# Zero-padded operands for two small matmuls, and weight rings of 3 and 5 buffers in place of 4 and 4

## Chip, core and metric

The kernel runs on one core of a Trainium2 chip. A core has five engines with a queue each: TensorE (PE, with PEld for its weight loads), VectorE (DVE), ScalarE (ACT), GpSimd (POOL) and SyncE (SP), which here only issues DMAs. The metric is the device time of one launch, the median of several runs.

## What is computed

One inference step of a two-layer decoder of width 2048, for 256 prompt tokens and 8 sequences of 8 new tokens ("sample"), 320 tokens in all, in float32. Layer 0 is gated linear attention with 4 heads, layer 1 is spatial gating; a squared-ReLU MLP of width 8192 and a LayerNorm follow each. What the change touches is, in the reference:

```python
# gated linear attention; per head a key width of 256 and a value width of 512
s_new = exp(b_last)[..., None] * s + einsum('bhsk,bhkv->bhkv', k_to_end, v)   # per sequence
# spatial gating over chunks of 128 positions, 8 groups of features
w_causal = where(causal, w_spatial, 0.0)
mixed = einsum('gts,bnsgd->bntgd', w_causal, v_chunks) + b_spatial
out = (u * mixed) @ w_out
```

## The kernel before

Activations lie feature-major: 16 tiles of 128 features, with the 320 tokens on the free axis. Every large product is made of three matmuls (`mm3`, L139 to L141), since each operand is split into an exact high part and a low part: low weights by high activations, high by low, high by high.

Weights come in **units** of 4 feature tiles by 256 columns (512 KB). There are 736 of them; each feeds 24 matmuls of 320 columns. `unit` issues the load on SP into `raw` (3 buffers), lets ACT write the high part `wh` (L128) and DVE the low part `wl` (L129):

```python
raw = wraw.tile([P, UK, UN], F32, tag="raw", ...)
hi = ring.pool.tile([P, UK, UN], F32R, tag="h" + ring.tag, ...)
lo = ring.pool.tile([P, UK, UN], F32R, tag="l" + ring.tag, ...)
...
nc.sync.dma_start(raw[:, ks, :], src[:, ks, :])                                  # L127
nc.scalar.copy(hi[:, ks, :], raw[:, ks, :])                                      # L128
nc.vector.tensor_sub(lo[:, ks, :], raw[:, ks, :], hi[:, ks, :].bitcast(F32))     # L129
```

`hi` and `lo` come from a **ring**, a pool whose buffers are used in turn: a unit can be cast when TensorE has done its last matmul on the unit that had the buffer. While the heads are at work there is one ring (pool `wa`, 4 buffers). When they are done (`second_half`), their tiles are given back, and a second ring (pool `wb`, 4 buffers) takes turns with the first for the rest of the program.

`group` makes two or four feature tiles of a product over all 16 feature tiles of the input, in PSUM banks called `mm`. **Side work** is handed out in steps between its units. For a head (`Head`) the order is: keys and queries together (8 units), values (8), the gate r (8). Beside r's units, and beside the next head's keys and queries, runs the attention itself, in four other PSUM banks called `gl`: `prompt_scores` (L461, L467), `prompt_o` (L482, L483), `prompt_state` (L498) and, for each of 8 sequences and 2 key tiles, `sample_step`: split a state tile into `sth` and `stl` (L537 on ACT, L538 on DVE), multiply the queries `qm` by both (L540, 128 rows by 512 columns), and work out what the state gains (L543) for DVE to add (L545). For L543 a sequence's keys are 32 rows of the tile `kts` (8 tokens by four parts) and its values the same 32 rows of `vts`, so the matmul contracts 32 rows:

```python
nc.tensor.matmul(pu[:], hd.kts[32 * i : 32 * (i + 1), g, kt * P : (kt + 1) * P],
                 hd.vts[32 * i : 32 * (i + 1), g, :], start=True, stop=True)     # L543
```

`kts` is written once for each key tile, by DVE (L382), from the transposed keys in a `gl` bank; ACT copies the prompt's part of that bank to `ktp` (L381). `qd`, `kte`, `kip`, `kis` (L359 to L386) are the decayed queries and keys that DVE makes out of the `mm` banks when keys and queries are there; they need the gates' exponents (`gate_logits`, `gate_sums`, `gate_decays`), a chain over TensorE, ACT and DVE that the first head has to wait for.

In layer 1, `mix` takes one of 16 feature tiles of v at a time: it transposes the two prompt blocks (L874) and the 64 sample tokens (L875), ACT copies them to `vt` (L878) and `vs` (L879), and TensorE multiplies them by the spatial weights `wsT` (L882, twice, float32) and by `wss` (L883), which holds the sample's 64 by 64 block-diagonal weights. Float32 matmuls are two matmuls each in the profile.

At the start POOL clears the tiles `scp`, `scs`, `scst` and `qm` (L230 to L237), and makes the identity and the causal masks (L210 to L222), which DVE turns into `mask_p` (L215) and `mask_s` (L227). x comes in pairs of feature tiles and is split as the weights are (`xh` L200, `xl` L201).

The order of the instructions on each engine is set by a scheduler that works on a model of the engines: it can put a unit's matmuls ahead of another's and moves side work between them. Waits between engines follow from the tiles.

Of the kernel before, what the change touches and what calls it, by code (L numbers as in the profile page):

```python
# [8 lines left out]
F32 = mybir.dt.float32  # L9
# [6 lines left out]
P = 128  # L16
D = 2048
KT = D // P          # feature tiles of a model-width activation
TP = 256             # prompt tokens
DB, DS = 8, 8        # sample batch and new tokens  # L20
T = TP + DB * DS     # tokens side by side on the free axis
TW = T + 2           # with two columns for the gain and the offset of a norm
H = 4
DK, DV = 256, 512
CH = 64              # GLA chunk
# [5 lines left out]
UK = 4               # k tiles in a weight unit  # L31
UN = 256             # columns in a weight unit
NU = KT // UK

# columns of the per-feature vectors
# [6 lines left out]
class Ring:  # L42
    """Where the split weight units of a GEMM live."""
# [5 lines left out]
class Side:  # L49
    """Work beside a GEMM, handed out in steps over the weight units still to come."""  # L50
# [16 lines left out]
def step_kernel(ctx: ExitStack, tc: tile.TileContext, A):  # L67
# [7 lines left out]
    # ------------------------------------------------------------ pools  # L75
# [3 lines left out]
    wa = ctx.enter_context(tc.tile_pool(name="wa", bufs=4))  # L79
# [9 lines left out]

    def mmtile(n=T):  # L90
        """Of the banks for products; two more of them once the heads are done."""
        if mx is not None:
            banks[0] = (banks[0] + 1) % 6
        return (mx if banks[0] > 3 else mm).tile([P, n], F32, tag="mm", name=nm("mm"), padded_shape=[P, 512])
# [4 lines left out]
    # ------------------------------------------------------------ constants  # L99
# [16 lines left out]
    # ------------------------------------------------------------ weights  # L116
    def unit(w, row0, q, col0, ring):
        """UK k tiles of UN columns, as exact high and low parts."""
# [5 lines left out]
        step = 2 if units[0] <= 2 else UK  # the first ones in parts, for an early start  # L124
# [18 lines left out]
    def group(w, row0, cols, rh, rl, evict, side=None, width=T, before=None):  # L143
        """Two feature tiles of w[row0:row0+D].T @ x for each of cols, k tiles outermost in units."""
# [15 lines left out]
    def rsqrt(out, src, scale, eps, eps_t, pool):  # L160
        """1 / sqrt(scale * src + eps): the table's value and a Newton step."""
# [10 lines left out]
    # ------------------------------------------------------------ layer 0: GLA  # L172
# [3 lines left out]
    def bigtile(tag, dt, name):  # L176
        """A model-wide activation in one of four buffers; b1 comes with the later pool."""
        return (lp if tag == "b1" else big).tile([P, KT, TW], dt, tag=tag, name=nm(name))

# [11 lines left out]
    # x, by k tiles, and its parts  # L191
    xT = A["xT"].rearrange("(k p) t -> p k t", p=P)
    def load_x(q):
        """x for quarter q of the features."""
# [12 lines left out]
    # causal masks: prompt [s of a 128-block, (t | t of the second block)]; sample [(i, part, s), (i', t)]  # L207
# [20 lines left out]
    # where the masked scores and the sample's queries go; what they leave is zero  # L228
# [5 lines left out]
    nc.gpsimd.memset(scst[:].bitcast(F32), 0.0)  # L234
    QW = P + DS
    qm = gp.tile([P, 2, DB * QW], F32R, tag="qm", name="qm")
    nc.gpsimd.memset(qm[:].bitcast(F32), 0.0)  # L237
    # per head: [1, d1, d1 d2 | 1, d2] for the queries, [d1 d2 d3, d2 d3, d3, 1] for the keys
# [8 lines left out]
    def load_gates():  # L247
        """The gate's weights; the second ones by 32 rows: high parts (twice), low parts."""
# [7 lines left out]
    def low_gate():  # L256
        """rows 0-15 x @ w_hi, rows 16-31 x @ w_lo, [hi | lo] side by side in the stationary operand; three times"""
# [22 lines left out]
    def bc4(ap):  # L280
        """[P, 64] sample columns -> [P, 8, 4, 8], the same for each part."""
        return ap.rearrange("p (b o t) -> p b o t", b=DB, o=1)
# [4 lines left out]
    class Head:  # L287
        """The gates of a head, its k, q and v, and what GLA reads of them."""
# [5 lines left out]
        def tiles(hd):  # L294
# [6 lines left out]
            hd.kts = gp.tile([P, 2, DK], F32R, tag="kts", name=nm("kts"))  # L301
# [3 lines left out]
        def gate_logits(hd):  # L305
            """exp(-|z|) and min(z, 0) of the logits z; a step for each table of ScalarE."""
# [12 lines left out]
        def gate_sums(hd):  # L319
            """log_sigmoid(z) = min(z, 0) - ln(1 + exp(-|z|)), summed along the chunks."""  # L320
# [35 lines left out]
        def ev_k(hd, kt, ps):  # L356
# [25 lines left out]
            nc.vector.tensor_copy(hd.kts[:, :, cs], pt[:, TP:].rearrange("p (b f) -> p b f", f=P))  # L382
# [31 lines left out]
        def project_kq(hd, side, before=None):  # L414
            """k and q together, as all four tiles of the other heads' work beside it are there."""
# [25 lines left out]
        def weigh(hd):  # L441
            """o * g * silu(r)"""
# [5 lines left out]
        def finish(hd):  # L448
            """... over the root of the mean square"""
# [4 lines left out]
        def prompt_scores(hd):  # L454
            """Scores of all chunk pairs at once, [s, t] for each block of 128 keys."""
# [64 lines left out]
        def sample_first(hd):  # L520
            """rows: 64 of the queries' high parts, 64 of the low ones"""
# [7 lines left out]
        def sample_step(hd, b, kt):  # L529
            """What state tile (b, kt) adds to o, and its update."""  # L530
# [8 lines left out]
            for part in (stl, sth):  # L539
# [3 lines left out]
            nc.tensor.matmul(pu[:], hd.kts[32 * i : 32 * (i + 1), g, kt * P : (kt + 1) * P],  # L543
                             hd.vts[32 * i : 32 * (i + 1), g, :], start=True, stop=True)
# [25 lines left out]
        def steps(hd):  # L570
            """GLA, by steps: the prompt at once, the sample's sequences one by one."""
# [22 lines left out]
    # ------------------------------------------------------------ the rest: residual stream z  # L594
# [7 lines left out]
    def second_half():  # L602
        """The heads are done: their tiles make room for the residual stream."""
# [10 lines left out]
        wb = ctx.enter_context(tc.tile_pool(name="wb", bufs=4))  # L614
# [408 lines left out]
```

## Time and profile before

| | before |
|---|---|
| time, median of 3 runs (lowest, highest) | 2784.06 us (2784.03, 2784.24) |
| span of the profiled execution | 2783.4 us |
| time around that span, against the median | 0.7 us |
| TensorE busy | 2763.0 us |
| DVE, ACT busy | 1543.0, 1179.7 us |
| mean granted TensorE clock | 0.999 |
| HBM read, written | 409.60, 22.02 MB |

In rows of groups, "128\*128" behind a matmul's tiles are its rows and columns of weights, "xN" the count, then the busy time and the mean length in ns, then the idle time of the engine ahead of them. In rows in order of time, the first number is the start from the span's begin and the second the length, both in us; a bracket tells of idle time ahead and what ended it. In rows of waits: who, for whom, us in total, times, longest.

The heads take the stretch from about 40 to 480 us, layer 0's products and MLP follow, `mix` runs between 1626 and 1705 us, and the rest is layer 1's products and MLP.

### The profile page before, as it was taken

The numbers are of one execution on the slowest core, as the hardware profiler recorded it, in microseconds if no ns is written. First come the engines' busy times: TensorE is split into PE (matmuls) and PEld (weight loads), VectorE is DVE, ScalarE is ACT, GpSimd is POOL, SyncE is SP. The second block draws the span as 40 slices with busy tenths as digits, with TensorE's granted clock in tenths as the row PEclk, the third lists the DMA queues.
The fourth block names the chain that finished last, engine by engine and source line by source line (L and its number), as shares of the span: only waits on it lengthen the run. The fifth ranks groups of instructions, "written<-read, shape, count | busy, mean of one in ns | idle before, by whom it ended". The sixth has DMA issues, their size and how long they took to land.

```text
span 2783.4 us, 44616 instructions
## 1 busy us (share of the span) xinstructions
PE 2763.0 (99%) x18493; PEld 2714.9 (98%) x18493; DVE 1543.0 (55%) x2276; ACT 1179.7 (42%) x1698; POOL 52.6 (2%) x83
## 2 busy tenths in 40 slices
PE   8999999999999999999999999999999999999998
PEld 8898998999999999999999999999999999999998
DVE  6566566886444444444468764587444444444446
ACT  5545454555334324323435553455324323423433
POOL 1000000000000000000000000000000000000001
PEclk9999999999999999999999999999999999999999
DMA  6556565654444445444445444445444444444442
GB/s 221 167 190 227 152 212 190 208 156 152 148 149 152 147 149 151 147 149 151 148 137 175 149 136 126 148 144 152 150 147 151 150 147 151 150 146 151 150 147 75
DMA packets 126396, 434.52 MB, mean 156 GB/s; under 512 B 13681, under 2 KB 17905, under 8 KB 126193
## 3 DMA queue, kind: packets, MB, share of 16 engines
q1 hardware_dynamic: 118800, 407.29, 47.3%
q0 software_dynamic: 6512, 23.20, 2.4%
q8 instruction: 144, 2.36, 0.3%
q10 hardware_dynamic: 880, 1.18, 0.1%
q14 instruction: 60, 0.48, 0.1%
HBM read 409.60 MB, written 22.02 MB: 155 GB/s over the span
## 4 chain that ended last, share of the span: by engine, by line
PE 98%; DVE 0%; ACT 0%; DMA 0%; issue 0%; SPq 0%; ACTq 0%; DVEq 0%
PE mm L139 31%; PE mm L141 31%; PE mm L140 31%; PE gl L540 1%; PE gl L543 1%; PE gl L498 1%; DMA xr<-xT 0%; PE gl L882 0%; PE gl L482 0%; PE gl L883 0%; ACT z L956 0%; DMA raw<-gla_w_in 0%; PE gl L874 0%; PE gl L483 0%; PE gl L409 0%
## 5 line engine op out<-in xcount | busy, mean ns | idle before, releaser
L129 DVE TENSOR_TENSOR wl<-raw,wh 128x1024 fp32r<-128x1024 f32 (+1 forms) x738 | 900.5, 1221 | 991.5 <-ACT wh L128 988.9
L128 ACT CAST wh<-raw 128x1024 fp32r<-128x1024 f32 (+1 forms) x738 | 771.4, 1046 | 1258.3 <-PE mm L141 1140.6
L141 PE MATMUL mm<-yh,wh 128*128 128x320 f32 x2368 | 734.0, 310 | 0.0
L140 PE MATMUL mm<-yl,wh 128*128 128x320 f32 x2368 | 732.4, 310 | 0.0
L139 PE MATMUL mm<-yh,wl 128*128 128x320 f32 x2368 | 727.8, 310 | 0.0
L141 PE MATMUL mm<-hh,wh 128*128 128x320 f32 x2048 | 635.3, 310 | 0.0
L139 PE MATMUL mm<-hh,wl 128*128 128x320 f32 x2048 | 634.4, 310 | 0.0
L140 PE MATMUL mm<-hl,wh 128*128 128x320 f32 x2048 | 633.6, 309 | 0.0
L140 PEld LDWEIGHTS mm<-yl,wh 128*128 128x128 f32 x2368 | 447.0, 189 | 0.2
L141 PEld LDWEIGHTS mm<-yh,wh 128*128 128x128 f32 x2368 | 446.1, 188 | 0.1
L139 PEld LDWEIGHTS mm<-yh,wl 128*128 128x128 f32 x2368 | 444.5, 188 | 0.0
L140 PEld LDWEIGHTS mm<-hl,wh 128*128 128x128 f32 x2048 | 386.7, 189 | 0.0
L141 PEld LDWEIGHTS mm<-hh,wh 128*128 128x128 f32 x2048 | 385.8, 188 | 0.0
L139 PEld LDWEIGHTS mm<-hh,wl 128*128 128x128 f32 x2048 | 385.8, 188 | 0.0
L139 PE MATMUL mm<-xh,wl 128*128 128x320 f32 x768 | 246.4, 321 | 9.7 <-ACT xh L200 5.8
L140 PE MATMUL mm<-xl,wh 128*128 128x320 f32 x768 | 241.1, 314 | 0.2 <-DVE xl L201 0.2
L141 PE MATMUL mm<-xh,wh 128*128 128x320 f32 x768 | 240.2, 313 | 0.0
L139 PEld LDWEIGHTS mm<-xh,wl 128*128 128x128 f32 x768 | 145.7, 190 | 22.1 <-issue 10.8
L140 PEld LDWEIGHTS mm<-xl,wh 128*128 128x128 f32 x768 | 146.3, 190 | 2.8 <-issue 1.4
L141 PEld LDWEIGHTS mm<-xh,wh 128*128 128x128 f32 x768 | 146.0, 190 | 2.2 <-issue 1.2
L792 ACT ACTIVATE r<-mm 128x320 f32<-128x320 f32 x120 | 52.6, 439 | 64.5 <-PE mm L141 64.5
L139 PE MATMUL mm<-ph,wl 128*128 128x320 f32 x256 | 78.9, 310 | 1.0 <-ACT ph L915 1.0
(272 smaller groups left out, 2493.5 us busy)
## 6 DMA issues: line engine op xcount, KB each, us to landing
raw<-mlp_w SPq DMA_DIRECT2D x512, 512.0 KB, 3.5
raw<-gla_w_in SPq DMA_DIRECT2D x94, 512.0 KB, 4.1
raw<-sg_w_in SPq DMA_DIRECT2D x64, 512.0 KB, 3.5
st<-state SPq DMA_DIRECT2D x32, 512.0 KB, 3.9
o_state_s<-st POOLq DMA_DIRECT2D x32, 512.0 KB, 3.8
raw<-gla_w_out SPq DMA_DIRECT2D x32, 512.0 KB, 4.3
raw<-sg_w_out SPq DMA_DIRECT2D x32, 512.0 KB, 3.6
z<-xT POOLq DMA_DIRECT2D x2, 1280.0 KB, 11.4
```

The costliest lines, as they stand in the source:

```text
L128: nc.scalar.copy(hi[:, ks, :], raw[:, ks, :])
L129: nc.vector.tensor_sub(lo[:, ks, :], raw[:, ks, :], hi[:, ks, :].bitcast(F32))
L139: nc.tensor.matmul(ps, wl[:, kk, s], x_h, start=first, stop=False)
L140: nc.tensor.matmul(ps, wh[:, kk, s], x_l, start=False, stop=False)
L141: nc.tensor.matmul(ps, wh[:, kk, s], x_h, start=False, stop=last)
L498: nc.tensor.matmul(pu[:], hd.ktp[:, blk, kt * P : (kt + 1) * P], hd.vtp[:, blk, :], start=(blk == 0), stop=(blk == 1))
L540: nc.tensor.matmul(po[:], qm[:, kt, b * P : (b + 1) * P], part[:], start=False, stop=(b == DB - 1 and kt == 1 and part is sth))
L543: nc.tensor.matmul(pu[:], hd.kts[32 * i : 32 * (i + 1), g, kt * P : (kt + 1) * P], hd.vts[32 * i : 32 * (i + 1), g, :], start=True, stop=True)
L792: nc.scalar.activation(r[:], ps[:], AF.Relu)
```

## The change

Four edits, with the lines of comment left out:

```diff
-    wa = ctx.enter_context(tc.tile_pool(name="wa", bufs=4))
+    wa = ctx.enter_context(tc.tile_pool(name="wa", bufs=3))
...
-        wb = ctx.enter_context(tc.tile_pool(name="wb", bufs=4))
+        wb = ctx.enter_context(tc.tile_pool(name="wb", bufs=5))
```

```diff
     nc.gpsimd.memset(scst[:].bitcast(F32), 0.0)
+    kz = gp.tile([P, 2, 4, DK], F32R, tag="kz", name="kz")
+    nc.gpsimd.memset(kz[:].bitcast(F32), 0.0)
...
-            hd.kts = gp.tile([P, 2, DK], F32R, tag="kts", name=nm("kts"))
...
             nc.scalar.copy(hd.ktp[:, :, cs], pt[:, 0:TP].rearrange("p (b f) -> p b f", f=P))
-            nc.vector.tensor_copy(hd.kts[:, :, cs], pt[:, TP:].rearrange("p (b f) -> p b f", f=P))
+            for i in range(4):
+                rows = slice(32 * i, 32 * (i + 1))
+                src = pt[rows, TP:].rearrange("p (b f) -> p b f", f=P)
+                if i % 2:
+                    nc.scalar.copy(kz[rows, :, i, cs], src)
+                else:
+                    nc.vector.tensor_copy(kz[rows, :, i, cs], src)
...
             pu = gltile()
-            nc.tensor.matmul(pu[:], hd.kts[32 * i : 32 * (i + 1), g, kt * P : (kt + 1) * P],
-                             hd.vts[32 * i : 32 * (i + 1), g, :], start=True, stop=True)
+            nc.tensor.matmul(pu[:], kz[:, g, i, kt * P : (kt + 1) * P], hd.vts[:, g, :], start=True, stop=True)
```

```diff
-        nc.vector.memset(wss[0:64], 0.0)
+        nc.vector.memset(wss, 0.0)
         for b in range(DB):
-            nc.gpsimd.dma_start(wss[DS * b : DS * (b + 1), :, DS * b : DS * (b + 1)], A["sg_wT"][0:DS, :, 0:DS])
-        nc.gpsimd.affine_select(out=wss[0:64], in_=wss[0:64], compare_op=ALU.is_ge, fill=0.0, base=0,
+            nc.gpsimd.dma_start(wss[64 + DS * b : 64 + DS * (b + 1), :, DS * b : DS * (b + 1)],
+                                A["sg_wT"][0:DS, :, 0:DS])
+        nc.gpsimd.affine_select(out=wss, in_=wss, compare_op=ALU.is_ge, fill=0.0, base=64,
                                 pattern=[[0, 8], [1, 64]], channel_multiplier=-1)
...
-        pt = gltile(T + 64)
-        for blk in range(2):
-            nc.tensor.transpose(pt[:, blk * P : (blk + 1) * P], v[:, j, blk * P : (blk + 1) * P], ident[:])
-        nc.tensor.transpose(pt[0:64, TP : TP + P], v[:, j, TP:T], ident[:])
-        vt = l2.tile([P, 2, P], F32, tag="vt", name=nm("vt"))
-        vs = l2.tile([64, P], F32, tag="vs", name=nm("vs"))
-        nc.scalar.copy(vt[:], pt[:, 0:TP].rearrange("p (b f) -> p b f", f=P))
-        nc.scalar.copy(vs[:], pt[0:64, TP : TP + P])
+        pt = gltile(3 * P)
+        for i, c0 in enumerate((0, P, T - P)):
+            nc.tensor.transpose(pt[:, i * P : (i + 1) * P], v[:, j, c0 : c0 + P], ident[:])
+        vt = l2.tile([P, 3, P], F32, tag="vt", name=nm("vt"))
+        nc.scalar.copy(vt[:], pt[:].rearrange("p (b f) -> p b f", f=P))
         pm = gltile(T)
         for blk in range(2):
             nc.tensor.matmul(pm[:, blk * P : (blk + 1) * P], vt[:, blk, :], wsT[:, g, :], start=True, stop=True)
-        nc.tensor.matmul(pm[:, TP:T], vs[:], wss[0:64, g, :], start=True, stop=True)
+        nc.tensor.matmul(pm[:, TP:T], vt[:, 2, :], wss[:, g, :], start=True, stop=True)
```

`kz` holds for each of the four sequences i of a group the keys in their own 32 rows and zeros in the other 96, so L543 (L551 in the changed kernel) contracts all 128 rows; it is cleared once and written by every head in the same places. In `mix` the third block now takes the last 128 tokens, the last half of the prompt's second block among them, and `wss` has zeros in the 64 rows that belong to these. The tile `ident_r` of the last norm takes the buffers of `vt` instead of `vs`.

The scheduler orders the changed kernel anew. TensorE, in the first step of the first head's sample, before (`wh_966` and `wl_967` are one weight unit):

```order
L540 MATMUL gl_903<-stl_957,qm 128x512
L540 MATMUL gl_903<-sth_956,qm 128x512
L543 MATMUL gl_962<-vts_522,kts_520 128x512
L141 MATMUL mm_855<-xh_88,wh_966 128x320
L139 MATMUL mm_855<-xh_88,wl_967 128x320
```

and now:

```order
L548 MATMUL gl_910<-stl_964,qm 128x512
L548 MATMUL gl_910<-sth_963,qm 128x512
L551 MATMUL gl_969<-vts_523,kz 128x512
L141 MATMUL mm_862<-xh_88,wh_973 128x320
L139 MATMUL mm_862<-xh_88,wl_974 128x320
```

Nothing moved here; the third row's operand is another. ACT, around the first head's gates (`wh` are casts of weight units, `eb` the gates' exponents), before:

```order
L537 CAST sth_995<-st_899 128x512
L128 CAST wh_485<-raw_484 128x1024 [waits DMAHW3_49,PE_49]
L274 CAST glow<-gl_284 96x320 [waits PE_49]
L128 CAST wh_566<-raw_565 128x1024 [waits DMAHW4_49,DVE_49,PE_49]
L128 CAST wh_596<-raw_595 128x1024 [waits DMAHW5_49,DVE_49,PE_49]
L314 ACTIVATE eb_350<-gl_352,vec 128x320 [waits DMASW0_49,PE_49]
L314 ACTIVATE eb_356<-gl_358,vec 128x320 [waits PE_49]
L317 ACTIVATE eb_350<-eb_350 128x320 [waits Activation_49]
```

and now:

```order
L128 CAST wh_457<-raw_456 128x1024 [waits DMAHW7_49,PE_49]
L277 CAST glow<-gl_286 96x320 [waits PE_49]
L128 CAST wh_487<-raw_486 128x1024 [waits DMAHW3_49,DVE_49,PE_49]
L316 ACTIVATE eb_352<-gl_354,vec 128x320 [waits DMASW0_49,PE_49]
L316 ACTIVATE eb_358<-gl_360,vec 128x320 [waits PE_49]
L128 CAST wh_573<-raw_572 128x1024 [waits DMAHW4_49,DVE_49,PE_49]
L319 ACTIVATE eb_352<-eb_352 128x320 [waits Activation_49]
```

Each cast of a unit stands one unit later against the gates: one cast less ahead of `glow`, and one between the two steps of the gates. DVE, at the very start (`wl` low weights, `xl` low parts of x), before:

```order
L129 TENSOR_TENSOR wl_148<-raw_146,wh_147 128x512 [waits DMAHW1_49,Activation_49]
L201 TENSOR_TENSOR xl_89<-xr_138,xh_88 128x2x320 [waits DMAHW0_49,Activation_49]
L215 CAST mask_p<-mf 128x384 [waits Pool_49]
L129 TENSOR_TENSOR wl_148<-raw_146,wh_147 128x512 [waits DMAHW2_49,Activation_49]
L225 TENSOR_TENSOR ms_110<-ms_110,ms_114 128x32 [waits Pool_49]
L201 TENSOR_TENSOR xl_89<-xr_142,xh_88 128x2x320 [waits DMAHW3_49,Activation_49]
L227 CAST mask_s<-ms_110 128x32 [waits DVE_49]
```

and now:

```order
L129 TENSOR_TENSOR wl_150<-raw_148,wh_149 128x512 [waits DMAHW1_49,Activation_49]
L201 TENSOR_TENSOR xl_89<-xr_140,xh_88 128x2x320 [waits DMAHW0_49,Activation_49]
L129 TENSOR_TENSOR wl_150<-raw_148,wh_149 128x512 [waits DMAHW2_49,Activation_49]
L201 TENSOR_TENSOR xl_89<-xr_144,xh_88 128x2x320 [waits DMAHW3_49,Activation_49]
L215 CAST mask_p<-mf 128x384 [waits Pool_49]
L201 TENSOR_TENSOR xl_89<-xr_181,xh_88 128x2x320 [waits DMAHW4_49,Activation_49]
L225 TENSOR_TENSOR ms_110<-ms_110,ms_114 128x32 [waits Pool_49]
L201 TENSOR_TENSOR xl_89<-xr_185,xh_88 128x2x320 [waits DMAHW6_49,Activation_49]
L227 CAST mask_s<-ms_110 128x32 [waits DVE_49]
L129 TENSOR_TENSOR wl_201<-raw_199,wh_200 128x512 [waits DMAHW0_49,Activation_49]
```

The three casts and sums of the masks moved behind two to three splits of x and weights. On SP the loads keep their order up to there.

More of the change, by code (lines that the diff above doesn't have):

```diff
@@ L924, in step_kernel @@
     ps = {}
-    ident_r = l2.tile([P, P], F32R, tag="vs", name="ident_r")
+    ident_r = l2.tile([P, P], F32R, tag="vt", name="ident_r")
     nc.scalar.copy(ident_r[:], ident[:])
```

## The prediction

> **What bounds the kernel.** I read the page first (busy times, the chain that ended last), then who TensorE waited for, then its instructions in order of time where the change touches them.
>
> ```profile
> span 2783.4 us, 44616 instructions
> PE 2763.0 (99%) x18493; PEld 2714.9 (98%) x18493; DVE 1543.0 (55%) x2276; ACT 1179.7 (42%) x1698; POOL 52.6 (2%) x83
> PE 98%; DVE 0%; ACT 0%; DMA 0%; issue 0%; SPq 0%; ACTq 0%; DVEq 0%
> ```
>
> TensorE carries 98% of the chain. What it waited for in all, longest first:
>
> ```profile
> PE mm L139 <- ACT xh L200: 5.8, 1, 5.8
> PE mm L139 <- DVE qd L386: 2.1, 1, 2.1
> PE mm L139 <- DVE wl L129: 1.8, 2, 1.3
> ```
>
> All of this lies in the first 46 us. So time is won or lost in two ways only: by what TensorE's instructions take from start to start, and by a new wait in front of them. A busy share of 99% doesn't say that each matmul is at its best. A matmul's row lasts longer than its turn, since the next one starts before it ends; I therefore read starts, not durations.
>
> **The state updates (L543).** One of them, by TensorE's instructions in order of time (start, length):
>
> ```profile
> L543 PE MATMUL gl<-vts,kts 32*128 32x512 f32 x64 | 26.7, 470 | 0.0
> ...
> 93.04 0.39 PE L540 MATMUL gl<-stl,qm 128*128 128x512 f32 x1
> 93.27 0.40 PE L540 MATMUL gl<-sth,qm 128*128 128x512 f32 x1
> 93.59 0.49 PE L543 MATMUL gl<-vts,kts 32*128 32x512 f32 x1
> 94.01 0.42 PE L139 MATMUL mm<-xh,wl 128*128 128x320 f32 x1
> 94.26 0.31 PE L140 MATMUL mm<-xl,wh 128*128 128x320 f32 x1
> 94.41 0.31 PE L141 MATMUL mm<-xh,wh 128*128 128x320 f32 x1
> ```
>
> Between operands of 128 rows a matmul of 512 columns takes 0.23 us from start to start (93.04 to 93.27) and one of 320 columns 0.15 (94.26 to 94.41). The one of 32 rows starts 0.32 after its forerunner instead of 0.23, is followed after 0.42 instead of 0.23, and the product behind it still takes 0.25 instead of 0.15. From 93.27 to 94.26 that is 0.99 where 0.23 + 0.23 + 0.15 = 0.61 would do: 0.38 us for going from 128 rows to 32 and back. When two updates stand together they share it:
>
> ```profile
> 99.21 0.40 PE L540 MATMUL gl<-sth,qm 128*128 128x512 f32 x1
> 99.54 0.73 PE L543 MATMUL gl<-vts,kts 32*128 32x512 f32 x2
> 100.20 0.41 PE L139 MATMUL mm<-xh,wl 128*128 128x320 f32 x1
> 100.45 0.40 PE L540 MATMUL gl<-stl,qm 128*128 128x512 f32 x1
> ```
>
> 1.24 us from 99.21 to 100.45, against 3 x 0.23 + 0.15 = 0.84: 0.40 for the place. And at two places the pair reads different groups of 32 rows:
>
> ```profile
> 463.40 0.31 PE L141 MATMUL mm<-xh,wh 128*128 128x320 f32 x1
> 463.64 0.50 PE L543 MATMUL gl<-vts,kts 32*128 32x512 f32 x2
> 464.07 0.42 PE L139 MATMUL mm<-xh,wl 128*128 128x320 f32 x1
> 464.32 0.31 PE L140 MATMUL mm<-xl,wh 128*128 128x320 f32 x1
> ```
>
> Both together take 0.43, so they run side by side: 0.92 from 463.40 to 464.32 against 0.15 + 2 x 0.23 + 0.15 = 0.76, a loss of only 0.16.
>
> TensorE's order has the 64 updates at 47 places, 30 single and 17 pairs, and the changed kernel has them at the same 47. With `kz` every update has 128 rows. Its price isn't in the trace; the nearest row is L540 of 128x512, at 0.23. Less can't be, as the same 512 columns stream; at most it stays as dear as now (no gain). I take 0.23: nothing then differs from L540. Saved: 45 x 0.39 + 2 x 0.16 = 17.9 us.
>
> A rule speaks against this. The Trainium skill, "TensorEngine Tiling (Array Packing)", section "Theoretical Speedup", promises up to 4x for a contraction of 32 rows or less by packing tiles side by side. An estimate by that page: the 64 updates packed in fours would take 64 x 0.23 / 4 = 3.7 us, padded ones 14.7, and the change would lose 11 us. The trace has this at 2 places of 47; that gain of 0.23 each is already inside the 0.16, so the sum doesn't change.
>
> **The mixing (L874 to L883).** One tile, in order of time, with the group of L882 ahead:
>
> ```profile
> L882 PE MATMUL gl<-bsp,vt 128*128 128x128 f32 x64 | 9.7, 274 | 0.0
> ...
> 1631.18 0.61 PE L882 MATMUL gl<-bsp,vt 128*128 128x128 f32 x4
> 1631.71 0.43 PE L883 MATMUL gl<-bsp,vs 64*128 64x64 f32 x2
> 1632.08 0.44 PE L874 MATMUL gl<-ident,v 128*128 128x128 f32 x2
> 1632.35 0.27 PE L875 MATMUL gl<-ident,v 128*64 128x128 f32 x1
> ```
>
> Four of L882 last 0.61 and one 0.274, so their starts lie (0.61 - 0.274) / 3 = 0.11 apart. From 1631.18 to 1632.35 eight instructions take 1.17; at 0.11 each they would take 0.88. The 0.29 goes with the 64 rows. The padded matmul (64 columns, 128 rows) lies between no gain and 0.11; I take 0.11, the price of its neighbours on the same weights' shape. 16 tiles x 0.29 = 4.6 us. The transpose of 128 columns in place of 64 takes the same turn. On ACT one copy of 384 columns stands for copies of 256 and 128; nobody waits for it on the chain.
>
> **Copies into `kz`.** Each of the 8 key tiles now has two copies on DVE and two on ACT, in place of one on DVE:
>
> ```profile
> L382 DVE CAST kts<-gl x8: 411/416/426, 57.7 to 400.5; 128x256 fp32r<-128x256 f32 x8
> L381 ACT COPY ktp<-gl x8: 366/372/376, 57.3 to 398.9; 128x256 f32<-128x256 f32 x8
> ```
>
> By these, 8 x 0.42 = 3.3 us more on DVE and 16 x 0.37 = 6 us more on ACT, spread over 350 us of a span in which DVE is busy 55% and ACT 42%. An estimate from the same rows: they hold one of the four `gl` banks some 1.2 us longer, three more copies of 0.4. The update shown at 93 us stands 35 us behind the first head's first copy at 57.7. I cost them at nothing; what hides them is the lead of the weights that ACT and DVE keep between the copies, and without that lead each would cost its 0.4 us, 24 x 0.4 = 9 us more.
>
> **The rings.** ACT fills a weight buffer when TensorE has left it, DVE writes the low part behind it. The longest such turn that I find beside the heads:
>
> ```profile
> ACT wh L128 <- PE mm L141: 1140.6, 504, 3.8
> ...
> 160.71 1.05 ACT L128 CAST wh<-raw 128x1024 fp32r<-128x1024 f32 x1 [1.74 <-PE mm L141]
> 164.29 1.05 ACT L128 CAST wh<-raw 128x1024 fp32r<-128x1024 f32 x1 [2.39 <-PE mm L141]
> ...
> 164.09 1.21 DVE L129 TENSOR_TENSOR wl<-raw,wh 128x1024 fp32r<-128x1024 f32 x1
> ```
>
> A unit lasts 3.6 us (160.71 to 164.29, both released by TensorE). The unit cast at 160.71 is complete at 165.30: a turn of 4.6. With four buffers TensorE has three units to work on meanwhile, 10.7 us; with three it has two, 7.2 us, and 2.6 are spare. So the ring of 3 costs nothing as long as a turn stays below 7.2. Later the rings of 3 and 5 alternate; the one of 3 lets its units start six ahead instead of eight, still 5 x 3.6 = 18 us of cover. I take 0; the bounds are 0 and, if the 8 units around a head's evictions came 0.5 us late, 4 heads x 8 x 0.5 = 16 us. A gain isn't in it, since a smaller ring only adds waits.
>
> **The start.** The memset of `kz` stands on POOL ahead of `qm`'s and of the masks:
>
> ```profile
> 3.44 1.93 POOL L237 MEMSET qm<- 128x2176 f32 x1
> ...
> 7.05 0.37 DVE L215 CAST mask_p<-mf 128x384 int32<-128x384 f32 x1 [0.18 <-POOL mf L212]
> ...
> 12.16 1.28 DVE L129 TENSOR_TENSOR wl<-raw,wh 128x512 fp32r<-128x512 f32 x2
> ...
> 12.90 0.41 PE L139 MATMUL mm<-xh,wl 128*128 128x320 f32 x1 [1.31 <-DVE wl L129]
> ```
>
> 2048 / 2176 x 1.93 = 1.8 us later come the masks. DVE's new order has `mask_p` two instructions later and `mask_s` right ahead of that `wl`, for which TensorE waits at 12.90. I take +0.1; bounds 0 and 1.8. The wait for `qd` remains, since the gates' chain of exponents is as long as before:
>
> ```profile
> 45.70 0.41 PE L139 MATMUL mm<-xh,wl 128*128 128x320 f32 x1 [2.08 <-DVE qd L386]
> ...
> 45.00:60.00 15.00, 14.30 (x87) 14.30 (x88) 10.29 (x34) 6.31 (x12) 0.00 (x0) 0.89 0.41 118
> ```
>
> The granted clock behind it is 0.89 over 15 us (the column behind POOL's), so 1.6 us are lost there; that loss may go, or double: +-1.6.
>
> **Sum.** -17.9 - 4.6 + 0.1 = -22.4 us. The profiled span of 2783.4 would become 2761.0; the runs' median is 2784.06, 0.7 above that span, so I predict 2761.7.
>
> **Rivals.** (a) The ring of 3 starves TensorE: a place beside the four heads, some 92 units, ACT's queue held by a cast that waits and the head's copies behind it. It decides when a turn exceeds 7.2 by 22.4 / 92 = 0.24 us in the mean; at 0.5 the time is 2784 - 22 + 46 = 2808. For it: DVE and ACT get more work in just those stretches. Against it: the longest turn is 4.6. Chance 4%. (b) The same, but only beside evictions: the 16 us above, or part of it, 2766 to 2778, chance 8%. (c) Only the gap around the small matmul goes, while the 0.10 of the product behind it belongs to something else: 47 x 0.10 = 4.7 less, 2766.4, chance 6%. (d) The change doesn't do what it says, since the gap has to do with the update's operands and not with its rows: only the mixing gains, 2779.5, within 0.2%; chance 2%. L883 with other operands shows the same gap, which speaks against it.
>
> **How the numbers follow.** 0.2% of 2784 is 5.6 us, about what a measurement of this kernel can tell from no change. My forecast has 80%: 2761.7, by itself from 2759 to 2764 (the clock's 1.6 and a few tenths at the start). The range to (b) and (c) is 2758 to 2771. Faster: 80 + 6 + 7 = 93%; same: (d) and the rest of (b), 3%; slower: 4%.
>
> **What would show it.** The updates at a mean near 395 ns instead of 470, with 0.23 from start to start and 0.15 behind them; L883's successor 0.11 behind its neighbours; TensorE's waits no longer than now. Wrong: waits of L139 or L140 for `wl` or `wh` after 50 us, or a product of 0.25 still standing behind each update.

## The result, and the profile after

The changed kernel takes 3016.81 us (median of 4 runs, 3007.51 to 3021.12), the one before 2784.15 beside it: a ratio of 1.0829 (95% interval 1.081 to 1.0848). The forecast was 2761.7. The profiled execution is the shortest of the four. From its page, the lines that answer to those shown of before:

```profile
span 3005.7 us, 44479 instructions
PE 2809.7 (93%) x18493; PEld 2746.4 (91%) x18493; DVE 1509.1 (50%) x2284; ACT 1157.1 (38%) x1698; POOL 54.7 (2%) x84
DMA 35%; PE 34%; DVE 13%; ACT 9%; issue 8%; ACTq 0%; SPq 0%; DVEq 0%
```

TensorE held 98% of the chain that ended last and holds 34% now; loads hold 35%, ACT and DVE together 22%. The waits after (who, for whom, us in total, times, longest):

```profile
ACT wh L128 <- DMA raw<-mlp_w: 1201.5, 251, 7.6
...
ACT wh L128 <- PE mm L141: 130.4, 62, 7.2
...
PE mm L139 <- DVE wl L129: 114.0, 121, 3.4
...
PE mm L139 <- ACT hh L794: 34.4, 6, 6.1
```

Before, ACT's casts waited 504 times for TensorE to leave a weight buffer. Now they wait for loads, and TensorE waits for the low weights, which is what the forecast named as the sign that it is wrong.

**The gain came.** The first single update and the first pair, in TensorE's order of time:

```profile
92.87 0.39 PE L548 MATMUL gl<-sth,qm 128*128 128x512 f32 x1
93.09 0.40 PE L551 MATMUL gl<-vts,kz 128*128 128x512 f32 x1
93.33 0.32 PE L139 MATMUL mm<-xh,wl 128*128 128x320 f32 x1
93.48 0.30 PE L140 MATMUL mm<-xl,wh 128*128 128x320 f32 x1
...
98.42 0.40 PE L548 MATMUL gl<-sth,qm 128*128 128x512 f32 x1
98.66 0.63 PE L551 MATMUL gl<-vts,kz 128*128 128x512 f32 x2
99.13 0.31 PE L139 MATMUL mm<-xh,wl 128*128 128x320 f32 x1
99.28 0.39 PE L548 MATMUL gl<-stl,qm 128*128 128x512 f32 x1
```

From 92.87 to 93.48 it is 0.61, where before it was 0.99; the pair takes 0.86 (98.42 to 99.28), where it was 1.24.

**Where the time went.** Each of the 736 units feeds 24 product matmuls, so the start of every 24th product gives TensorE's place in the program. The difference to the kernel before, in us (below zero: ahead of it), in the profiled executions; the other kernels are those of the experiments:

| unit | changed | 3 and 5 alone | 3 and 5, raw 4 | 3 and 3 | by turns of 8 | ring of 3 first |
|---|---|---|---|---|---|---|
| 20 | -1.1 | -1.9 | -1.6 | -1.2 | -3.2 | -2.7 |
| 100 | -17.6 | -1.9 | -1.6 | -17.7 | -19.7 | -19.2 |
| 108 | -13.8 | 3.7 | 3.5 | -13.3 | -15.8 | -19.5 |
| 180 | -13.8 | 3.7 | 3.5 | -13.3 | -15.9 | -19.3 |
| 250 | 20.1 | 35.1 | 3.5 | -13.3 | -16.0 | -19.5 |
| 380 | 95.0 | 113.9 | 3.5 | -13.3 | -16.2 | -20.1 |
| 420 | 97.6 | 115.3 | 3.5 | -13.3 | -16.2 | -20.1 |
| 450 | 103.2 | 124.8 | 3.5 | -18.6 | -21.6 | -25.6 |
| 540 | 105.9 | 126.8 | 3.5 | -18.6 | -21.6 | -25.9 |
| 735 | 222.4 | 236.1 | 3.5 | -18.6 | -21.9 | -26.7 |

The updates gain 16.5 us from unit 20 to 100. 3.8 are lost where the second ring opens (units 100 to 108). From unit 180 on 236.2 are lost, nearly all in two stretches, 180 to 380 and 540 to 735. Both are long products with little side work. The same stretch of time, before and then after (us, busy time and instructions of PE, PEld, DVE, ACT, POOL, granted clock, DMA share, GB/s):

```profile
771.00:1479.00 708.00, 708.00 (x4805) 708.00 (x4804) 336.30 (x407) 258.90 (x324) 0.00 (x0) 1.00 0.49 149
```

```profile
771.00:1479.00 708.00, 632.71 (x4126) 614.09 (x4125) 260.88 (x310) 210.47 (x272) 0.00 (x0) 0.98 0.40 129
```

The loads don't move more, they move less. The view of the tile `raw` in that window tells what the casts waited for, before:

```profile
L128 ACT CAST wh<-raw x200: 1032/1050/1056, 771.5 to 1475.7; 128x1024 fp32r<-128x1024 f32 x100
...
  PE mm L141: 392.5, 166
...
  DMA raw<-mlp_w: 5.6, 4
...
DMA to landing us min/median/max: 3.3/3.5/5.4
```

and after:

```profile
L128 ACT CAST wh<-raw x174: 1034/1048/1053, 770.1 to 1474.3; 128x1024 fp32r<-128x1024 f32 x174
...
  DMA raw<-mlp_w: 451.3, 85
...
  PE mm L141: 10.7, 2
...
DMA to landing us min/median/max: 3.4/3.8/5.8
```

174 units in 708 us are 87 pairs of 8.14 us each; TensorE needs 7.08 for a pair (200 units before). 85 of the 87 pairs wait for a load. The loads come in twos now, and the median of 3.8 mixes two kinds. By the trace's records of the units 188 to 361, cast in this window, the first of two lands after 3.5 us (median), as before, and the second, issued 1.1 us behind it, after 4.5. So the loads start too late, and the second, for which the casts wait, takes 1 us longer as well.

**One turn of the loop.** ACT, DVE, TensorE and SP, the changed kernel, in order of time each:

```profile
802.69 2.00 ACT L128 CAST wh<-raw 128x1024 fp32r<-128x1024 f32 x2 [6.52 <-DMA raw<-mlp_w]
810.53 2.00 ACT L128 CAST wh<-raw 128x1024 fp32r<-128x1024 f32 x2 [5.84 <-DMA raw<-mlp_w]
818.62 2.00 ACT L128 CAST wh<-raw 128x1024 fp32r<-128x1024 f32 x2 [6.09 <-DMA raw<-mlp_w]
...
811.61 2.36 DVE L129 TENSOR_TENSOR wl<-raw,wh 128x1024 fp32r<-128x1024 f32 x2 [5.48 <-ACT wh L128]
...
814.03 0.42 PE L139 MATMUL mm<-yh,wl 128*128 128x320 f32 x1 [0.53 <-DVE wl L129]
822.12 0.41 PE L139 MATMUL mm<-yh,wl 128*128 128x320 f32 x1 [0.76 <-DVE wl L129]
```

```profile
805.02 0.33 SPq L127 DMA_DIRECT2D raw<-mlp_w  x1
806.16 0.33 SPq L127 DMA_DIRECT2D raw<-mlp_w  x1
812.87 0.33 SPq L127 DMA_DIRECT2D raw<-mlp_w  x1
814.00 0.33 SPq L127 DMA_DIRECT2D raw<-mlp_w  x1
```

Number the units in the order of their loads, odd ones in the ring of 3, even ones in the ring of 5; the program's order of casts on ACT tells which is which. Units 197 and 198 are loaded at 805.02 and 806.16, 199 and 200 at 812.87 and 814.00. The casts come in pairs, an even unit three ahead of the odd one: (196, 193) at 802.69, (198, 195) at 810.53, (200, 197) at 818.62. The loop is seen from 810.53: DVE is through with 198 and 195 at 813.97 (811.61 + 2.36), which gives back two raw buffers; the second of the loads that this lets go is unit 200's, issued at 814.00; its cast starts at 818.62, 4.62 later. 3.44 + 0.03 + 4.62 = 8.09 us for a pair, one behind the other. The view of the DMAs (KB each, median us from issue to landing) has for the loads issued at 812.87 and at 814.00:

```profile
raw<-mlp_w SPq DMA_DIRECT2D x1, 512.0 KB, 3.5
```

```profile
raw<-mlp_w SPq DMA_DIRECT2D x1, 512.0 KB, 4.5
```

With 3.5 us for the second load too, the loop would take 3.44 + 0.03 + 3.5 = 7.0 us, an estimate from these rows: a little less than TensorE's 7.08. By that estimate the loop is slower than TensorE only because both loads of a pair are let go together; no run tried this by itself.

What makes it a loop is unit 197. By the trace's records its data have landed at 808.53, and TensorE has left its weight buffer (unit 191's) at 801.49. It could be cast then. But 200 stands ahead of it in ACT's queue, so it is cast at 819.57, 11 us later, and TensorE, which needs it next, starts on it 0.05 us after its low part is there (822.12). Unit 200, for which all of them waited, is used at 834.03, 13 us after its casts. And as long as 197 sits in `raw`, only two of the three raw buffers turn over, so that 200's load could not start sooner. (By the kernel's instructions the raw buffers aren't used strictly in turn: a load gets one that the scheduler's model has free, and 200 has the one that 195 had.) The Trainium skill, "PSUM — Partial Sum Buffer", section "Engine vs sequencer instructions", says that the queues of ScalarE and VectorE are strictly first in, first out; this trace agrees, with those 11 us.

### The profile page after: what moved, and what is told of

Read it like the earlier page. It is cut to its first block, busy times and chain, and to the rows that moved or that the text cites. A ratio compares the mean times of both kernels' runs of the same rounds, so it can differ in the third digit from the quotient of the medians.

```text
span 3005.7 us, 44479 instructions
## 1 busy us (share of the span) xinstructions
PE 2809.7 (93%) x18493; PEld 2746.4 (91%) x18493; DVE 1509.1 (50%) x2284; ACT 1157.1 (38%) x1698; POOL 54.7 (2%) x84
## 3 DMA queue, kind: packets, MB, share of 16 engines
q8 instruction: 144, 2.36, 0.3%
## 4 chain that ended last, share of the span: by engine, by line
DMA 35%; PE 34%; DVE 13%; ACT 9%; issue 8%; ACTq 0%; SPq 0%; DVEq 0%
DMA raw<-mlp_w 31%; DVE wl L129 11%; PE mm L139 10%; PE mm L140 10%; PE mm L141 10%; ACT wh L128 9%; DMA raw<-sg_w_in 2%; DMA raw<-sg_w_out 2%; PE gl L548 1%; DVE f L793 1%; PE gl L551 0%; PE gl L506 0%; DVE dgl L684 0%; DMA xr<-xT 0%; PE gl L490 0%
## 5 line engine op out<-in xcount | busy, mean ns | idle before, releaser
L129 DVE TENSOR_TENSOR wl<-raw,wh 128x1024 fp32r<-128x1024 f32 (+1 forms) x738 | 884.6, 1219 | 1327.6 <-ACT wh L128 1326.0
L128 ACT CAST wh<-raw 128x1024 fp32r<-128x1024 f32 (+1 forms) x738 | 753.3, 1045 | 1520.2 <-DMA raw<-mlp_w 1201.5
L139 PE MATMUL mm<-yh,wl 128*128 128x320 f32 x2368 | 741.5, 316 | 88.0 <-DVE wl L129 88.0
L139 PE MATMUL mm<-hh,wl 128*128 128x320 f32 x2048 | 646.3, 316 | 59.8 <-ACT hh L794 34.4
L140 PE MATMUL mm<-hl,wh 128*128 128x320 f32 x2048 | 642.6, 314 | 3.2 <-DVE hl L795 2.6
L141 PE MATMUL mm<-hh,wh 128*128 128x320 f32 x2048 | 642.0, 314 | 0.0
L139 PEld LDWEIGHTS mm<-hh,wl 128*128 128x128 f32 x2048 | 392.8, 192 | 69.6 <-ACT hh L794 36.0
L140 PEld LDWEIGHTS mm<-hl,wh 128*128 128x128 f32 x2048 | 393.4, 192 | 6.4 <-DVE hl L795 6.4
L141 PEld LDWEIGHTS mm<-hh,wh 128*128 128x128 f32 x2048 | 392.6, 192 | 0.0
L139 PEld LDWEIGHTS mm<-xh,wl 128*128 128x128 f32 x768 | 146.2, 191 | 13.6 <-ACT xh L200 6.0
L794 ACT CAST hh<-f 128x320 fp32r<-128x320 f32 x128 | 58.3, 459 | 87.1 <-DVE f L793 86.9
```

The costliest lines, as they stand in the source:

```text
L139: nc.tensor.matmul(ps, wl[:, kk, s], x_h, start=first, stop=False)
L140: nc.tensor.matmul(ps, wh[:, kk, s], x_l, start=False, stop=False)
L141: nc.tensor.matmul(ps, wh[:, kk, s], x_h, start=False, stop=last)
L794: nc.scalar.copy(hh[:, j, 0:T], f[:])
```

## The experiments

The theory on record, "parked loads": rings of 3 and 5 used alternately make the scheduler cast out of the order of the loads, and what is loaded and not cast takes the raw buffers from the loads. How far the orders differ is read from the kernels' instructions (units overtaken by later ones in ACT's order of casts, of 736) and stands in the last column. Each ratio is to the kernel before, timed beside it (2784.15 to 2785.02 us).

| label | kernel | us | ratio to before (95%) | overtaken by 1, by 2 |
|---|---|---|---|---|
| (before) | rings 4 and 4, 3 raw | 2784.15 | 1 | 7, 3 |
| (changed) | padding, rings 3 and 5 | 3016.81 | 1.0829 (1.081 to 1.0848) | 58, 251 |
| pad_rings_3_3 | padding, rings 3 and 3 | 2766.12 | 0.9933 (0.9918 to 0.9947) | 7, 2 |
| rings_3_5_alone | no padding, rings 3 and 5 | 3019.39 | 1.0844 (1.0828 to 1.086) | 57, 252 |
| rings_3_5_raw4 | the same, 4 raw | 2788.85 | 1.0014 (1.0005 to 1.0024) | 13, 299 |
| pad_3_5_by_turns_of_8 | padding, 3 and 5, in turns of 8 | 2763.39 | 0.9923 (0.9906 to 0.994) | 8, 0 |
| pad_rings_3_4 | padding, rings 3 and 4 | 2766.20 | 0.9933 (0.9919 to 0.9946) | 299, 3 |
| raw2_rings_4_4 | no padding, 4 and 4, 2 raw | 2795.96 | 1.004 (1.0027 to 1.0054) | 4, 0 |
| raw2_rings_3_4 | no padding, 3 and 4, 2 raw | 3036.82 | 1.0898 (1.0881 to 1.0915) | 246, 0 |
| mixing_alone | padded mixing only, 4 and 4 | 2779.84 | 0.9982 (0.9973 to 0.999) | 7, 3 |
| rings_3_5_by_turns_alone | no padding, 3 and 5, in turns of 8 | 2787.62 | 1.0011 (1.0002 to 1.002) | 8, 0 |
| updates_alone_by_turns | padded updates only, 3 and 5, in turns of 8 | 2770.55 | 0.9949 (0.9937 to 0.9962) | 8, 0 |
| pad_3_5_ring3_first | padding, 3 and 5, other phase of 8 | 2758.89 | 0.9911 (0.9898 to 0.9925) | 9, 0 |

**pad_rings_3_3**

```diff
-        wb = ctx.enter_context(tc.tile_pool(name="wb", bufs=5))
+        wb = ctx.enter_context(tc.tile_pool(name="wb", bufs=3))
```

> The changed kernel with its second ring at 3 buffers instead of 5: both rings are even again, and both shallow; the padding stays. Theory 'parked loads': with rings of 3 and 5 the casts go in another order than the loads (a unit of the ring of 5 is cast ahead of the older one of the ring of 3), so a loaded unit of the ring of 3 sits in one of the three raw buffers for a pair and a half, and the next two loads can start only when a pair has been cast. A pair then takes a load of two units (4.3 us from issue to landing) plus its casts (about 3.5 us), some 8 us instead of the 7.08 that TensorE needs. With even rings the casts follow the order of the loads, so this kernel should need 2762 us (2759 to 2768), 8% less than the changed one. Rival 'shallow ring': a ring of 3 gives too little lead; then two of them are at least as slow as 3017. Rival 'padding': the copies into kz disturb the casts for good; then it stays near 3017.

2766.12 us. Two weight buffers fewer take 250 us off. So neither the ring of 3 as such nor the padding makes the loss.

**rings_3_5_alone**

```diff
# the kernel before
-    wa = ctx.enter_context(tc.tile_pool(name="wa", bufs=4))
+    wa = ctx.enter_context(tc.tile_pool(name="wa", bufs=3))
...
-        wb = ctx.enter_context(tc.tile_pool(name="wb", bufs=4))
+        wb = ctx.enter_context(tc.tile_pool(name="wb", bufs=5))
```

> The kernel before, without any padding, with the rings of 3 and 5. 'Parked loads' and 'shallow ring' both expect the whole loss: the changed kernel lost 233 us net against the kernel before and had gained about 22 by the padding, so 2784 + 255 = 3039 us (3025 to 3050). 'Padding' expects 2784.

3019.39 us (3018.05 to 3022.64): the rings alone make the loss, and the padding is not needed for it. The size was missed by 20 us: I had added the padding's whole gain. In the profiled executions the two kernels are 17.5 us apart at unit 180 and 13.7 at the end, though the mixing lies between; in their medians it is 2.6. What a stretch loses when loads set its pace differs from one execution to the next (the changed kernel's runs lie 13.6 us apart), and it isn't settled how much of the padding's gain is really absorbed there.

**rings_3_5_raw4**

```diff
# on top of rings_3_5_alone
-    wraw = ctx.enter_context(tc.tile_pool(name="wraw", bufs=3))
+    wraw = ctx.enter_context(tc.tile_pool(name="wraw", bufs=4))
```

> The same (no padding, rings of 3 and 5) with 4 raw buffers instead of 3. The casts still go out of the order of the loads, one unit overtaken by two later ones, as with 3 raw buffers. 'Parked loads': with one raw buffer more, the load of the next unit of the ring of 5 starts when the previous such unit is cast (1.05 + 1.2 us), so the loop is 2.3 + 3.5 (one load) = 5.8 us per pair, less than the 7.08 that TensorE needs; the loss goes, 2784 us (2782 to 2792). 'Shallow ring' and a fourth theory, 'order of casts' (the casts of the ring of 5 stand ahead of those of the ring of 3 in ACT's and DVE's queues, and that alone makes the ring of 3 late, whatever the loads do), expect no help: about 3039.

2788.85 us: one raw buffer takes back 230.5 of 234.8. The order of casts is as bad as before (299 units overtaken by two, 3 more by three). What is left is lost where the second ring opens (units 100 to 108 in the table of differences); behind that the kernel stays 3.5 us behind the one before, so disorder alone costs nothing. ACT in the same stretch of the program:

```profile
803.25 1.05 ACT L128 CAST wh<-raw 128x1024 fp32r<-128x1024 f32 x1 [2.49 <-PE mm L141]
806.78 1.05 ACT L128 CAST wh<-raw 128x1024 fp32r<-128x1024 f32 x1 [2.48 <-PE mm L141]
```

Each cast waits for TensorE again, 3.53 apart, and no longer for a load.

**pad_3_5_by_turns_of_8**

```diff
-        return rings[turn[0] % len(rings)]
+        return rings[turn[0] % 8 not in (0, 3, 6)] if len(rings) > 1 else rings[0]
```

> The changed kernel with its rings of 3 and 5 used in a pattern of eight units, three from the ring of 3 and five from the ring of 5, instead of alternately; every buffer then comes up once in eight units. Nothing else differs. 'Parked loads': the casts follow the order of the loads, so the loss goes: 2762 us (2759 to 2768). 'Shallow ring': the ring of 3 is now asked three times in eight units instead of four, which leaves at least half of the loss: over 2880. 'Padding': 3017.

2763.39 us. The same buffers as in the changed kernel, 253 us less: with three units of eight in the ring of 3 and five in the ring of 5 each buffer comes free in the order of the loads.

**pad_rings_3_4**

```diff
-        wb = ctx.enter_context(tc.tile_pool(name="wb", bufs=5))
+        wb = ctx.enter_context(tc.tile_pool(name="wb", bufs=4))
```

> The changed kernel with rings of 3 and 4. The casts are out of the loads' order for nearly as much of the program as with 3 and 5, but a unit of the ring of 3 is overtaken by one later unit at most places, nowhere by two for long. 'Parked loads': the next unit of the longer ring is then already being loaded while a pair is cast; the loop is one cast and one load, 2.3 + 3.5 = 5.8 us per pair, less than 7.08, and no time is lost: 2764 us (2761 to 2769). A theory that any disorder costs, in proportion to how far it goes ('order of casts'), expects about half the loss, 2880. 'Shallow ring' has been answered by the rings of 3 and 3.

2766.20 us. It isn't a matter of degree: 299 units overtaken by one cost nothing with 3 raw buffers, 251 overtaken by two cost all. Its waits show a few loads that came late, and none of it reached TensorE:

```profile
ACT wh L128 <- PE mm L141: 1096.9, 483, 7.4
ACT wh L128 <- DMA raw<-mlp_w: 55.0, 28, 3.8
```

**raw2_rings_4_4**

```diff
# the kernel before
-    wraw = ctx.enter_context(tc.tile_pool(name="wraw", bufs=3))
+    wraw = ctx.enter_context(tc.tile_pool(name="wraw", bufs=2))
```

> The kernel before with 2 raw buffers instead of 3, rings of 4 and 4, casts in the order of the loads. 'Parked loads': a raw buffer is taken for a load (3.5 to 4.3 us) and its casts (2.3 us), 5.8 to 6.6 us in all, and comes up once in two units, 7.08 us; so no time is lost: 2784 to 2790 us. If two free raw buffers are too few in any order, it loses, 2850 or more.

2795.96 us, 6 above the expected range. By units 3.3 us are lost at the start and 8.4 between units 100 and 140, where norms are worked out; from unit 140 to 735 the difference stays at 11.7 to 11.8. In the long products two raw buffers are enough when they turn over in order.

**raw2_rings_3_4**

```diff
# on top of raw2_rings_4_4
-    wa = ctx.enter_context(tc.tile_pool(name="wa", bufs=4))
+    wa = ctx.enter_context(tc.tile_pool(name="wa", bufs=3))
```

> The same with 2 raw buffers, rings of 3 and 4, no padding. Each unit of the ring of 3 is overtaken by one later unit, at 246 places. 'Parked loads': with 2 raw buffers that one parked unit is as bad as two overtakings are with 3: both loads of a pair can start only when the pair before is cast, some 8.1 us instead of 7.08; 2784 + 246 x 1.0 = 3030 us (2990 to 3070). If being overtaken by one is harmless in itself, it stays near the kernel with 2 raw buffers and even rings.

3036.82 us, as expected (3030). The overtaking by one that was free with three raw buffers costs 241 us with two. The waits are those of the changed kernel:

```profile
ACT wh L128 <- DMA raw<-mlp_w: 1242.3, 275, 8.1
PE mm L139 <- DVE wl L129: 123.3, 130, 3.1
```

So the loss was taken away in four ways (even rings, rings nearer to each other, another raw buffer, another pattern of turns) and made anew with other numbers.

**mixing_alone**, the kernel before with the third part of the change's diff and nothing else; one line of it:

```diff
...
-        nc.tensor.matmul(pm[:, TP:T], vs[:], wss[0:64, g, :], start=True, stop=True)
+        nc.tensor.matmul(pm[:, TP:T], vt[:, 2, :], wss[:, g, :], start=True, stop=True)
...
```

> The kernel before with the padded mixing alone (L874 to L883 and wss), rings of 4 and 4, updates of 32 rows. The term of the forecast: 16 x 0.29 = 4.6 us less, 2779.5 (2778.5 to 2781). If the rows of 64 aren't the cause of the gap, 2784.

2779.84 us, 5.2 less than before beside it; by units, 5.4 between 420 and 450.

**rings_3_5_by_turns_alone**, the kernel before with rings of 3 and 5 and the line of pad_3_5_by_turns_of_8:

```diff
# on top of rings_3_5_alone
-        return rings[turn[0] % len(rings)]
+        return rings[turn[0] % 8 not in (0, 3, 6)] if len(rings) > 1 else rings[0]
```

> The kernel before, no padding, with rings of 3 and 5 in the pattern of eight units (three from the ring of 3, five from the ring of 5). What is left of the rings' cost when no load is parked: in the other kernels with 3 buffers beside the heads TensorE falls back by 4 to 5 us between units 100 and 108, where the second ring opens, with the padding and without it. So 2784.5 + 4 = 2788.5 us (2787 to 2791). If that loss goes with the padding's copies and not with the ring of 3, 2784.5.

2787.62 us. Between units 100 and 108 it loses 4.1 us, with no padding: the place where the second ring opens has to do with the ring of 3.

**updates_alone_by_turns**, pad_3_5_by_turns_of_8 with the mixing of before; one line of it:

```diff
# on top of pad_3_5_by_turns_of_8
...
-        nc.tensor.matmul(pm[:, TP:T], vt[:, 2, :], wss[:, g, :], start=True, stop=True)
+        nc.tensor.matmul(pm[:, TP:T], vs[:], wss[0:64, g, :], start=True, stop=True)
...
```

> The padded updates (kz) without the padded mixing, rings of 3 and 5 in the pattern of eight units. By the forecast's term the updates gain 17.9 us; the ring of 3 costs about 4 where the second ring opens: 2784.5 - 17.9 + 4 = 2770.6 us (2767 to 2772).

2770.55 us. Against the kernel that differs by the updates alone it is 17.1 less (2787.62 - 2770.55).

**pad_3_5_ring3_first**

```diff
# on top of pad_3_5_by_turns_of_8
-        return rings[turn[0] % 8 not in (0, 3, 6)] if len(rings) > 1 else rings[0]
+        return rings[turn[0] % 8 not in (1, 2, 3)] if len(rings) > 1 else rings[0]
```

> The whole padding, with another phase of the pattern of eight: where the second ring opens, the next three units that TensorE works on come from the ring of 3, the ones behind them from the ring of 5, whose buffers lie in memory that the last head gives up only then. If the loss of 4 us at that place is TensorE waiting for the first units in the new ring, it shrinks to 0 to 2: 2760.5 us (2759 to 2762.5), the best of all. If it is the one unit less of lead that a ring of 3 has, in any phase, it stays at 2763.4.

2758.89 us (2758.5 to 2763.73), the best of all, just under the expected range and 26.1 below before. The lost 4 us are seen in pad_3_5_by_turns_of_8, ACT, DVE, TensorE, and the window behind the wait (columns as above):

```profile
471.61 2.95 ACT L128 CAST wh<-raw 128x1024 fp32r<-128x1024 f32 x3 [3.35 <-DVE o_all L454]
474.57 1.28 ACT L164 ACT_TABLE_LOAD   x1
475.87 0.53 ACT L164 ACTIVATE ny<-gl,eps_h 128x320 f32<-128x320 f32 x1
...
476.43 0.49 DVE L165 TENSOR_SCALAR nw<-gl 128x320 f32<-128x320 f32 x1 [0.24 <-ACT ny L164]
...
476.97 0.42 PE L139 MATMUL mm<-oh,wl 128*128 128x320 f32 x1 [2.54 <-DVE nw L165]
```

```profile
477.00:482.00 5.00, 5.00 (x23) 5.00 (x24) 3.92 (x6) 3.14 (x3) 0.00 (x0) 0.66 0.73 261
```

The wait of 2.54 ends with L165, a step of the last head's norm that reads a `gl` bank, and not with low weights. By the kernel's instructions TensorE goes on to unit 104, whose product takes over that very bank; 104 is the second of the three casts, and by the trace's records its low part is there at 475.05. The first of the three is unit 102. It goes into the new ring and starts when DVE is done with L454, the last head's weighing (3.35 us of waiting), and the norm's L164 stands behind all three on ACT. After the wait the granted clock is 0.66 for 5 us, and unit 104 takes 5.18 us (476.97 to 482.15) where it took 3.64 before; with the wait, which was 0.27 before, that makes 3.8 us.

In the other phase units 102 and 103 lie in the new ring and 104 in the ring of 3; 104 is cast first of three, from 469.30, L165 ends at 474.77, and TensorE starts on 104 at 474.82 without a wait. From unit 100 to 108 it even gains 0.3. The forecast of this run had the place and the remedy right; what TensorE waited for was the bank and not the new ring's first unit.

## Why the prediction was wrong, step by step

- **The rings, "I take 0": this step failed.** The prediction reckoned how long a weight buffer's turn is, found 18 us of cover for the ring of 3, and stopped there. The cover is there: even rings of 3 and 3 lose nothing from unit 108 on. What it didn't follow is the buffer ahead of the ring. Units leave `raw` in the order of the casts, and the casts' order comes from when the scheduler's model has each ring's buffers free: a unit of the ring of 3 can be cast when the unit six before it is done, one of the ring of 5 when the unit ten before it is. That difference of four units parks a loaded unit, and 3 raw buffers are then one too few. (The counts of the table fit this: with 3 and 4 buffers, where the difference is two, units are overtaken by one, with 3 and 5 by two, with even rings or turns of eight hardly any.) The cover of 18 us is gone then: a loop of loads and casts gives TensorE a pair of units in 8.1 us where it needs 7.08. It cost 236 us in the profiled execution, the shortest, and 253 by the medians (3016.81 against 2763.39 in turns of eight), where the prediction's bound was 16.
- **Rival (a), "the ring of 3 starves TensorE"**, had the right sign and the right waiter, 4% and 2808. Its place was wrong (beside the heads nothing is lost, units 20 to 100), and so was its cause, a turn longer than 7.2 us. **Rival (b)**, late weights beside evictions, wasn't seen. Something of its size came at one place, the opening of the second ring (3.8 us), but there the profile names the norm's L165 (2.5 us of waiting in the changed kernel too) and not the weights.
- **The updates, -17.9:** right. 0.61 and 0.86 at the two places shown, where 0.61 and 0.84 were reckoned; 17.1 by two kernels that differ in nothing else. Starts of 0.23 came as foretold, the mean length didn't (417 ns, not near 395: lengths overlap, and a row's length is no turn). **Rival (c)** is out, as the product behind now takes 0.15, and so is **(d)**.
- **The mixing, -4.6:** a little too small; 5.2 and 5.4. In pad_3_5_by_turns_of_8 the padded matmul of 64 columns (L888) has these rows:

```profile
1624.61 0.61 PE L887 MATMUL gl<-bsp,vt 128*128 128x128 f32 x4
1625.06 0.33 PE L888 MATMUL gl<-bsp,vt 128*128 128x64 f32 x2
...
L888 PE MATMUL gl<-bsp,vt 128*128 128x64 f32 x32 | 5.3, 249 | 0.0
```

  0.33 for two and 0.249 for one are 0.08 from start to start, not the 0.11 of its neighbour of 128 columns: 32 x 0.03 = 1.0 us more.
- **The copies into `kz`, 0:** nothing seen of them. In units 20 to 100 the kernels with the copies gain 16.5, and three of the 47 places, at some 0.39 each, lie ahead of unit 20.
- **The start, +0.1, and the clock, +-1.6:** at unit 0 the changed kernel is 0.2 late. The stretch from 45 to 60 us has a granted clock of 0.89 in it too, and 1.00 in pad_3_5_by_turns_of_8, which is 2.1 us ahead of it at unit 20.

Without the failed step the time is near the forecast of 2761.7: 2763.39 with the rings in turns of 8, and 2758.89 with their phase shifted. That the first comes so near is in part luck. By the table of differences its profiled execution is 3.2 us ahead at unit 20, where +0.1 +-1.6 were reckoned, and loses 3.9 at the opening of the second ring, which wasn't reckoned at all. The updates and the mixing themselves are right by the kernels that have them alone.

## What to carry to other kernels

Where several pools feed one consumer through one staging pool, let every buffer come up in the order of the loads: use pools of n and m buffers n and m times in a round of n + m (tried here with 3 and 5 alone), or make them equal. When a change touches a pool's depth, write down, from the new order of each engine, which load waits for which cast and how many staging buffers are held by units that are loaded and not yet cast; a lead of many units in the weights says nothing about the loads behind them. And a wait at the head of an in-order queue is to be judged by what is queued behind it: here ACT stood 6 us of every 8 before a unit that was needed 13 us later, with the one that was needed at once behind it.

## What the runs showed of the hardware

A load of 512 KB takes 3.5 us from issue to landing (median before); when two are issued 1.1 us apart, the second's data are there for ACT after 4.6 (814.00 to 818.62). The Trainium skill, "DMA: Bandwidth & Descriptors", section "Anatomy of one DMA — SWDGE (gpsimd) path", gives for DMAs that GpSimd issues some 2.0 us that don't depend on the size; an estimate by its fit would be 3.2 us for 512 KB. The loads here are issued by SP, for which that section gives no fit, and no run here splits their 3.5 us.

The four runs of the kernel before lie within 0.1% of each other (2784.03 to 2786.45), those of the changed kernel, whose pace is set by the loop of loads and casts, 0.45% apart (3007.51 to 3021.12). In the stretch from 771 to 1479 us the granted clock was 1.00 with TensorE always busy, and 0.98 with a pause in every pair. A lower clock with less work was unexpected; what it costs there, where loads set the pace, was not tried by itself.
